# Triangular inverses of an RWKV-7 trunk layer: blocks of 16 joined to 32 by TensorE in place of blocks of 32 by substitution

## The chip, the cores and the metric

The kernel runs on one core of one Trainium2 chip. The metric is the device time of one execution in microseconds (us); the kernel before was run three times. Names of engines: TensorE (PE, with its weight loads as PEld), VectorE (DVE), ScalarE (ACT), GpSimd (POOL), SyncE (SP, which issues the DMAs).

## What is computed

One layer of a hybrid trunk on 128 context tokens and 512 latent tokens, width 1024: an input projection, a bidirectional RWKV-7 time mixing with 8 heads of 64 beside a grouped-query attention with 8 heads of 64, one output projection, and a gated feed-forward with a convolution of width 3. What this case is about is the time mixing:

```python
def wkv_scan(r, w, k, v, kk, a, s0, reverse):
    def step(s, inp):
        r_t, w_t, k_t, v_t, kk_t, a_t = inp
        sa = jnp.einsum('bhvk,bhk->bhv', s, -kk_t)
        s = (s * w_t[:, :, None, :]
             + sa[..., None] * (kk_t * a_t)[:, :, None, :]
             + v_t[..., None] * k_t[:, :, None, :])
        return s, jnp.einsum('bhvk,bhk->bhv', s, r_t)
```

It runs once forwards and once backwards over the tokens. The outputs are the two token streams, the new keys and values of the context and the final states.

## The kernel before

The scan is done in chunks of 64 tokens. Within a chunk the step's rank-one corrections form a strictly triangular 64 x 64 matrix L for each chunk, head and direction, and the chunk needs the inverse of (1 - L). The rest of a chunk is matmuls. There are three groups of such matrices: G0 and G1, each two pairs of heads over the 8 latent chunks, and CX, all four pairs over the 2 context chunks. A "unit" is one chunk and pair in one direction; a group has `nu` units per direction, 16 in G0 and G1 and 8 in CX. Two heads of a pair lie on partitions 0 to 63 and 64 to 127, so the tile `LT` of a group is 128 partitions x 32 units x 64.

`inverse` (L829) does a group in three stages:

- Blocks onto rows. Each 64 x 64 matrix has two diagonal blocks of 32. VectorE transposes in four instructions (L845), one per 32 partitions, so that each partition holds one unit's block of 32 x 32. L854 adds the block to its transpose, so that forward and backward units look alike.
- Substitution. L870 and L871 make the inverse of the 32 x 32 blocks, all 128 at once, column by column: 30 pairs of a product and a sum. They run on VectorE for G0 and CX and on POOL for G1 (`EN_INV`). Twelve small ScalarE copies (L858 to L864) set the start. Two VectorE transposes (L875, L877) bring the inverses back as `XT` and `XN`.
- Join to 64. TensorE makes W = L X and B = X W with matmuls of 32 x 32 x 32, each in its own quarter of rows (L897, L898, L909, L910), and copies put the blocks into `MT`.

The work around it: the front (`s_lora`, `s_kk`, `s_prep`, `s_bonus`) makes decays and keys beside the input projection (`s_gemm`, L502 and L521); `s_prep` ends with the matmuls `lt` (L819) and their masked copies into `LT` (L823). Then `s_gemm2` does the gate (L556) and the q projections (L570) while `s_gram`, `s_decay` and `s_chain` (L1042 to L1115) run the two scan directions; attention (`s_norm`, `s_scores`, `s_attn`) begins when the q projections and the inverse of G1 are through. The scans and the attention share TensorE; then come the output projection and the feed-forward.

What sets the order: every such function is a stream. `Flow` (L272) is a planner that takes, step by step, the stream that can start first by its estimated costs (`T` for TensorE, `V`, `A`, `G`) and priorities, with rings that count free PSUM banks; each `yield` names an engine and a cost. The order that comes out is fixed in the program, and each engine works through its own in order. PSUM rings used here: `mi` (2 banks; front, grams and decays, and the inverse of G0), `md` (1 bank), `tm` (3 banks; gate and q projections).

Of the kernel before, what the change touches and what calls it, by code (L numbers as in the profile page):

```python
# [9 lines left out]
F32 = mybir.dt.float32  # L10
# [3 lines left out]
ALU = mybir.AluOpType  # L14
# [5 lines left out]
P = 128  # L20
# [27 lines left out]
def trunk(ctx: ExitStack, tc: tile.TileContext, a, o, dbg=None):  # L48
# [8 lines left out]
    def nm(s):  # L57
        uid[0] += 1
        return f"{s}_{uid[0]}"
# [62 lines left out]
    qkn = rc.tile([P, 2, 64], F32, name="qkn")  # L122
    gnw = rc.tile([P, 4, 64], F32, name="gnw")
    bia = cst.tile([P, 4], F32, name="bia")
# [93 lines left out]
    sy.dma_start(qkn, a["qkn"].to_broadcast([P, 2, 64]))  # L218
    for h in range(2):
        sy.dma_start(gnw[64 * h:64 * h + 64], a["gnw"][h:h + 1].to_broadcast([64, 4, 64]))  # L220
    e2 = [psa.two("b2", "fm") for _ in range(2)]
# [50 lines left out]
    class Flow:  # L272
# [12 lines left out]
        def ring(f, name, n):  # L285
            f.rings[name] = [f.now] * n
# [95 lines left out]
    def ev_(*key):  # L382
        return ("ev", key)
# [444 lines left out]

    def inverse(g, en, pl, mp, sfx, rg, bank):  # L829
        eng = ve if en == "V" else ge  # L830

        def W(n, k=1):
            return V(n, k=k) if en == "V" else G(0.99 * (k * 0.1 + 2.2e-3 * n))
# [5 lines left out]
        yield ring("inv" + sfx)  # L839
        Lt = pl.tile([P, 1024], F32, name=nm("Lt"), tag="i0" + sfx)  # L840
        for qd in range(4):
            pr = slice(32 * qd, 32 * qd + 32)
            t0 = 32 * (qd % 2)
            yield V(1024)
            ve.transpose(Lt[pr].rearrange("p (t s) -> p t s", s=32), LT[pr, :, t0:t0 + 32].rearrange("p u t -> p t u"))  # L845
        Ls = pl.tile([P, 32, 32], F32, name=nm("Ls"), tag="i1" + sfx)
        X = pl.tile([P, 1024], F32, name=nm("X"), tag="i2" + sfx)
        X3 = X.rearrange("p (t s) -> p t s", s=32)
        Lt3 = Lt.rearrange("p (t s) -> p t s", s=32)
        yield G(1.0)  # L850
        ge.memset(X, 0.0)
        ge.memset(X[:, ::33], 1.0)
        yield W(1024)
        eng.tensor_tensor(Ls, Lt3, Lt3.rearrange("p t s -> p s t"), ALU.add)  # L854

        yield A(496, k=12)
        Lf = Ls.rearrange("p t s -> p (t s)")
        se.copy(X[:, 32::66], Lf[:, 32::66])  # L858
        for i in range(2):
            for j in range(2):  # L860
                se.copy(X[:, 64 + 32 * i + j::132], Lf[:, 64 + 32 * i + j::132])
        for b in (4, 8, 16):
            for q in range(0, 32, 2 * b):
                se.copy(X3[:, q + b:q + 2 * b, q:q + b], Ls[:, q + b:q + 2 * b, q:q + b])  # L864
        tmp = pl.tile([P, 256], F32, name=nm("tmp"), tag="i3" + sfx)
        for s in range(1, 31):
            n = 31 - s
            yield W(2 * n * s, k=2)
            t3 = tmp[:, :n * s].rearrange("p (t j) -> p t j", j=s)
            eng.tensor_tensor(t3, Ls[:, s + 1:32, s:s + 1].to_broadcast([P, n, s]), X3[:, s:s + 1, 0:s].to_broadcast([P, n, s]), ALU.mult)  # L870
            eng.tensor_tensor(X3[:, s + 1:32, 0:s], X3[:, s + 1:32, 0:s], t3, ALU.add)  # L871
        XT = pl.tile([P, 1024], F32, name=nm("XT"), tag="i0" + sfx)
        XN = pl.tile([P, 1024], F32, name=nm("XN"), tag="i1" + sfx)
        yield V(1024)
        ve.transpose(XT, X)  # L875
        yield V(1024)
        ve.transpose(XN.rearrange("p (j u) -> p j u", u=32), X3.rearrange("p i j -> p j i"))  # L877
        XT3 = XT.rearrange("p (i u) -> p u i", u=32)
        XN3 = XN.rearrange("p (j u) -> p u j", u=32)
        MT = mp[0].tile([P, 2 * nu, 64], F32, name=nm("MT"), tag=mp[1] or "MT" + g.nm)  # L880
        g.MT = MT
# [616 lines left out]
    weights = [flow.add(3, s_wload(1, jobs1 + jobs2, wpool, 2), 0), flow.add(3, s_wsplit(1, jobs1 + jobs2, wpool, 2), 0)]  # L1498
    flow.add(1.2, inverse(G0, "V", ri, (ri, None), "", "mi", mi), B_I0)
    flow.run([flow.add(2, s_gemm())])  # L1500
# [36 lines left out]
    for d in range(2):  # L1537
        rwkv += [flow.add(pri, st_(d), {s_chain: B_CH, s_load: 200, s_gram: 100, s_decay: 50}[st_]) for pri, st_ in ((0, s_chain), (0.1, s_load), (0.2, s_gram), (0.2, s_decay))]
    flow.add(PR_INV[0], inverse(CX, EN_INV[0], ri, (rp2, None), "", "md", md), B_INV)
    ipp = pool("ip", side="left")  # L1540
    inv1 = flow.add(PR_INV[1], inverse(G1, EN_INV[1], ipp.__enter__(), (ri, "LTg0"), "x", "md", md), B_INV)
    rwkv += [flow.add(0.5, s_setup(), 100), flow.add(0.75, s_final(), B_FIN)]
# [673 lines left out]
```

## Time and profile before

| | |
|---|---|
| runs | 1106.88, 1106.60, 1103.13 us; median 1106.6 |
| the profiled execution | 1104.36 us |
| its span, first to last instruction | 1102.6 us |
| TensorE busy | 1019.5 us (92%), mean granted clock 0.94 |
| VectorE busy | 790.7 us (72%) |
| ScalarE busy | 563.4 us (51%) |
| POOL busy | 507.4 us (46%) |

An engine's busy time is the union of its instructions; matmuls are pipelined and their ends are modelled, so a busy TensorE is not always one at its peak. The granted clock is TensorE's: 1.00 is 2.4 GHz, 0.50 is 1.2 GHz, and a mean between mixes the two. A matmul of f32 operands stands in the trace as two records. The columns of each view are named where it first appears.

### The profile page before, as it was taken

The numbers are of one execution on the slowest core, as the hardware profiler recorded it, in microseconds if no ns is written. First come the engines' busy times: TensorE is split into PE (matmuls) and PEld (weight loads), VectorE is DVE, ScalarE is ACT, GpSimd is POOL, SyncE is SP. The second block draws the span as 40 slices with busy tenths as digits, with TensorE's granted clock in tenths as the row PEclk, the third lists the DMA queues.
The fourth block names the chain that finished last, engine by engine and source line by source line (L and its number), as shares of the span: only waits on it lengthen the run. The fifth ranks groups of instructions, "written<-read, shape, count | busy, mean of one in ns | idle before, by whom it ended". The sixth has DMA issues, their size and how long they took to land. (4 is left out here: it accounts for less than half of the span.)

```text
span 1102.6 us, 20567 instructions
## 1 busy us (share of the span) xinstructions
PE 1019.5 (92%) x8034; PEld 853.6 (77%) x8034; DVE 790.7 (72%) x1367; ACT 563.4 (51%) x1261; POOL 507.4 (46%) x446
## 2 busy tenths in 40 slices
PE   6999998778779999999999988999999998899997
PEld 3788776677665556777777888999999997788885
DVE  3536689989729777465774789999999999643324
ACT  4275433254654767476654764555555556334431
POOL 1234423567415204210202058788888888642330
PEclk8899998889857899799999999999999999899999
DMA  9414534640245684211061421222222223531202
GB/s 364 185 67 116 152 103 133 184 126 21 97 150 194 212 267 136 68 59 61 9 229 74 153 90 44 88 89 94 77 77 78 78 99 112 193 113 58 95 1 96
DMA packets 70433, 127.84 MB, mean 116 GB/s; under 512 B 15664, under 2 KB 41776, under 8 KB 67264
## 3 DMA queue, kind: packets, MB, share of 16 engines
q1 hardware_dynamic: 70336, 126.53, 34.4%
q8 instruction: 63, 1.03, 0.4%
q14 instruction: 34, 0.28, 0.1%
HBM read 105.00 MB, written 21.51 MB: 115 GB/s over the span
## 5 line engine op out<-in xcount | busy, mean ns | idle before, releaser
L1807 POOL TENSOR_TENSOR w<-raw,w 128x512 fp32r<-128x512 f32 (+1 forms) x84 | 153.9, 1839 | 142.6 <-ACT w L1806 121.4
L2050 PE MATMUL dn<-w,ah 128*128 128x512 f32 x660 | 155.7, 398 | 7.9 <-DVE c L1850 7.9
L2050 PEld LDWEIGHTS dn<-w,ah 128*128 128x128 f32 x660 | 125.1, 190 | 38.3 <-issue 8.3
L1844 PE MATMUL up<-tq,w 128*128 128x324 f32 x960 | 150.2, 312 | 2.8 <-DVE x L1989 2.8
L1844 PEld LDWEIGHTS up<-tq,w 128*128 128x128 f32 x960 | 145.2, 190 | 3.1 <-DVE x L1989 3.1
L1844 PE MATMUL up<-hq,w 128*128 128x324 f32 x864 | 137.0, 313 | 4.8 <-ACT w L1806 2.3
L1844 PEld LDWEIGHTS up<-hq,w 128*128 128x128 f32 x864 | 129.6, 188 | 7.8 <-DVE up L1992 4.6
L1807 POOL TENSOR_TENSOR w<-sw,w 128x512 fp32r<-128x512 f32 x80 | 122.4, 1551 | 8.6 <-ACT w L1806 8.6
L1924 DVE TENSOR_TENSOR ah<-act,ah 128x644 fp32r<-128x644 f32 x42 | 58.7, 1415 | 75.8 <-ACT ah L1923 75.8
L1848 ACT ACTIVATE c<-up,pv 128x322 f32<-128x322 f32 x86 | 52.1, 620 | 97.3 <-DVE up L1992 55.6
L432 POOL TENSOR_TENSOR lo<-raw,hi 128x1024 fp32r<-128x1024 f32 x17 | 42.7, 2509 | 68.4 <-ACT hi L430 66.9
L1063 POOL TENSOR_TENSOR SP<-vse,pt 64x128 f32<-64x128 f32 x36 | 14.3, 398 | 128.4 <-DVE vse L1113 127.7
L1923 ACT CAST ah<-act 128x644 fp32r<-128x644 f32 x44 | 31.8, 732 | 76.4 <-PE dn L2050 76.3
L1806 ACT CAST w<-raw 128x512 fp32r<-128x512 f32 (+1 forms) x86 | 63.2, 748 | 5.0 <-PE dn L2050 2.8
L964 PE MATMUL gr<-AK 64*128 64x128 f32 x320 | 47.4, 329 | 11.8 <-ACT DT L377 4.5
L964 PEld LDWEIGHTS gr<-AK 64*128 64x128 f32 x320 | 38.8, 222 | 21.4 <-ACT DT L377 4.7
L1687 PE MATMUL op<-wo,m 128*128 128x512 f32 x192 | 48.3, 404 | 1.7 <-DVE m L1681 1.0
L1849 DVE SCALAR_TENSOR_TENSOR c<-up,pv,c 128x322 f32<-128x322 f32 x86 | 46.5, 543 | 3.8 <-ACT c L1848 3.8
L1806 ACT CAST w<-sw 128x512 fp32r<-128x512 f32 x80 | 47.5, 620 | 2.7 <-PE up L1844 2.7
L1850 DVE SCALAR_TENSOR_TENSOR c<-up,pv,c 128x322 f32<-128x322 f32 x86 | 46.6, 545 | 0.8
L1687 PEld LDWEIGHTS op<-wo,m 128*128 128x128 f32 x192 | 36.7, 194 | 10.5 <-DVE m L1681 1.4
L968 DVE TENSOR_TENSOR GM<-gr,cm 128x512 f32<-128x512 f32 x40 | 26.8, 684 | 21.7 <-PE gr L964 21.3
(335 smaller groups left out, 2485.1 us busy)
## 6 DMA issues: line engine op xcount, KB each, us to landing
wm<-in_wmod SPq DMA_DIRECT2D x24, 1024.0 KB, 6.6
raw<-in_up SPq DMA_DIRECT2D x44, 512.0 KB, 3.3
raw<-in_down SPq DMA_DIRECT2D x22, 512.0 KB, 3.3
AK<-arkd SPq DMA_DIRECT2D x40, 256.0 KB, 4.4
raw<-in_wfm SPq DMA_DIRECT2D x10, 512.0 KB, 5.9
arkd<-AR SPq DMA_DIRECT2D x8, 640.0 KB, 3.7
xT<-in_xT SPq DMA_DIRECT2D x8, 320.0 KB, 6.1
arkd<-BK SPq DMA_DIRECT2D x16, 160.0 KB, 3.5
```

What stands on the lines that cost most here:

```text
L432: ge.tensor_tensor(lo, raw, hi.bitcast(F32), ALU.subtract)
L964: te.matmul(ps[par][:, s, i], lhsT=ak[pr, i, 1], rhs=ak[pr, i, 0], start=True, stop=True)
L1687: te.matmul(acc[hf], lhsT=m2[xi][:, k - k0], rhs=wo[k // 2][wi][k % 2][:, 512 * hf:512 * hf + 512], start=(n_mm == 0 and pi == 0), stop=(n ...
L1806: se.copy(hi, raw)
L1807: eng.tensor_tensor(lo, raw, hi.bitcast(F32), ALU.subtract)
L1844: te.matmul(ps, lhsT=wq[wi][:, 128 * k:128 * k + 128], rhs=xq[xi][:, k], start=(first and k == 0 and pi == 0), stop=(last and k == 3 and p ...
L1848: se.activation(c, src[..., 1:H2N - 1], AF.Identity, scale=pv[:, col + 1:col + 2], bias=pv[:, col + 3:col + 4])
L1849: ve.scalar_tensor_tensor(c, src[..., 0:H2N - 2], pv[:, col:col + 1], c, ALU.mult, ALU.add)
L1850: ve.scalar_tensor_tensor(c, src[..., 2:H2N], pv[:, col + 2:col + 3], c, ALU.mult, ALU.add)
L1923: se.copy(t[:, 0, 1:645], act[:, k, 1:645])
L1924: eng.tensor_tensor(t[:, 1, 1:645], act[:, k, 1:645], t[:, 0, 1:645].bitcast(F32), ALU.subtract)
L2050: return [te.matmul(ps, lhsT=(ah, al)[xi][:, p0:p0 + 128], rhs=w2[wi][:, k % 2], start=(k == 0 and pi == 0), stop=(k == 21 and pi == 2)) f ...
```

## The change

The blocks that are inverted by substitution are now 16 x 16, two per old block of 32.

- Blocks onto rows: 128 matmuls per group (after.py L855) of 32 rows and 16 columns against a piece of the identity, in four quarters, into one PSUM bank `Lp`; ScalarE copies it (L863) and VectorE adds the transpose (L865), masks with a new constant `low` (L868) and sets the ones (L869).
- Substitution: 14 pairs (L875, L876), each on the two blocks of a partition at once.
- Join to 32: `T` (L895, L897), 4 matmuls per unit and direction; ScalarE copies `Ts` (L899); `D` (L911), 8 matmuls of 16 columns per unit and direction; VectorE adds them into `XN` and `XT` (L914, L915), the first through a row mask `m16`. The join to 64 stays.
- The second bank ring of an inverse is `mi` for G0 and `tm` for CX and G1.
- `low` lies where `gnw` lay; `gnw` is loaded in `s_final`, when `low` is free.

```diff
+    low = rc.tile([P, 4, 64], F32, name="low", tag="gnw").rearrange("p a (b s) -> p (a b) s", s=16)
+    ge.memset(low, 0.0)
+    for t in range(1, 16):
+        ge.memset(low[:, t, 0:t], 1.0)
+    m16 = rc.tile([P, 1], F32, name="m16")
+    ve.tensor_reduce(m16, ident.rearrange("p (q h x) -> p q h x", q=4, h=2)[:, :, 1], AX.XY, ALU.add)
...
-        for qd in range(4):
-            pr = slice(32 * qd, 32 * qd + 32)
-            t0 = 32 * (qd % 2)
-            yield V(1024)
-            ve.transpose(Lt[pr].rearrange("p (t s) -> p t s", s=32), LT[pr, :, t0:t0 + 32].rearrange("p u t -> p t u"))
...
+        quads = [(slice(32 * qd, 32 * qd + 32), slice(32 * qd, 32 * qd + 16), 32 * (qd % 2)) for qd in range(4)]
+        yield ring(rl)
+        Lp = lbank("Lt").rearrange("p (b t s) -> p b t s", b=2, s=16)
+        for t in range(32):
+            if t % 8 == 0:
+                yield T(0.6)
+            b = t // 16
+            for pr, _, t0 in quads:
+                c = pr.start + 16 * b
+                te.matmul(Lp[pr, b, t % 16], lhsT=LT[pr, :, t0 + t], rhs=ident[pr, c:c + 16], start=True, stop=True)
...
-        yield W(1024)
-        eng.tensor_tensor(Ls, Lt3, Lt3.rearrange("p t s -> p s t"), ALU.add)
-
-        yield A(496, k=12)
...
-        for s in range(1, 31):
-            n = 31 - s
-            yield W(2 * n * s, k=2)
...
+        yield A(512)
+        se.copy(Ls, Lp)
+        yield V(512)
+        ve.tensor_tensor(Ls, Ls, Lp.rearrange("p b t s -> p b s t"), ALU.add)
+        flow.give(rl)
+        yield V(544, k=2)
+        ve.tensor_tensor(Xb, Ls, low[:, None].to_broadcast([P, 2, 16, 16]), ALU.mult)
+        ve.memset(X[:, 0:1024:33], 1.0)
+        tmp = pl.tile([P, 112], F32, name=nm("tmp"), tag="i3" + sfx)
+        for s in range(1, 15):
+            n = 15 - s
+            yield W(4 * n * s, k=2)
...
+        Ts = pl.tile([P, 2 * nu, 32], F32, name=nm("Ts"), tag="i2" + sfx)
+        for h, rr, bb in ((0, rg, bank), (1, rl, lbank)):
+            yield ring(rr)
+            T3 = bb("T")[:, :32 * nu].rearrange("p (u j) -> p u j", j=32)
+            for u in range(h * nu, h * nu + nu):
+                if u % 8 == 0:
+                    yield T(0.5)
+                for pr, hr_, t0 in quads:
+                    if h:
+                        te.matmul(T3[pr, u - nu], lhsT=LT[pr, u, t0:t0 + 32], rhs=XT3[pr, u], start=True, stop=True)
+                    else:
+                        te.matmul(T3[pr, u], lhsT=LT[hr_, u, t0:t0 + 32], rhs=XN3[hr_, u], start=True, stop=True)
+            yield A(32 * nu)
+            se.copy(Ts[:, h * nu:h * nu + nu], T3)
+            flow.give(rr)
+        for h, rr, bb in ((0, rg, bank), (1, rl, lbank)):
+            yield ring(rr)
+            D3 = bb("D")[:, :32 * nu].rearrange("p (u w j) -> p u w j", w=2, j=16)
+            for u in range(h * nu, h * nu + nu):
+                if u % 8 == 0:
+                    yield T(1.0)
+                for pr, hr_, _ in quads:
+                    k = hr_ if h else pr
+                    ops = (((Ts[k, u], XN3[k, u, 0:16]), (XN3[k, u], Ts[k, u, 16:32])) if h else ((XT3[k, u], Ts[k, u, 0:16]), (Ts[k, u], XT3[k, u, 16:32])))
+                    for w, (l_, r_) in enumerate(ops):
+                        te.matmul(D3[pr, u - h * nu, w], lhsT=l_, rhs=r_, start=True, stop=True)
+            us = slice(h * nu, h * nu + nu)
+            yield V(32 * nu, k=2)
+            ve.scalar_tensor_tensor(XN3[:, us, 0:16], D3[:, :, 0], m16, XN3[:, us, 0:16], ALU.mult, ALU.add)
+            ve.tensor_tensor(XT3[:, us, 16:32], XT3[:, us, 16:32], D3[:, :, 1], ALU.add)
+            flow.give(rr)
...
+        gnw = rc.tile([P, 4, 64], F32, name="gnw", tag="gnw")
+        for h in range(2):
+            sy.dma_start(gnw[64 * h:64 * h + 64], a["gnw"][h:h + 1].to_broadcast([64, 4, 64]))
```

The order moves in three places that matter here. In these rows a name is that of a tile, "x16" counts equal instructions, and the shape at the end is that of the output.

TensorE at the end of the front, before: after the last piece of the k and v projection (`tm`) come the LT matmuls of the last head pair and then the gate (`fm`).

```order
L521 MATMUL tm_1814<-hi_1827,hhi 128x256
L521 MATMUL tm_1814<-hi_1827,hlo 128x256
L521 MATMUL tm_1814<-lo_1828,hhi 128x256
L819 MATMUL lt_1666<-AR_1606,BK_1607 64x64 x16
L819 MATMUL lt_1707<-AR_1606,BK_1607 64x64 x4
L819 MATMUL lt_1721<-AR_1661,BK_1662 64x64 x16
L819 MATMUL lt_1747<-AR_1661,BK_1662 64x64 x4
L556 MATMUL fm_2143<-hhi,hi_2025 128x320
```

The same place now (L518 is the projection, L816 `lt`, L734 the decays' matmul `lo`):

```order
L518 MATMUL tm_2445<-hi_2449,hlo 128x256
L518 MATMUL tm_2445<-lo_2450,hhi 128x256
L897 MATMUL T_1513<-XN_1456,LT_507 32x32 x64
L895 MATMUL T_1600<-XT_1455,LT_507 32x32 x64
L911 MATMUL D_1679<-Ts_1512,XT_1455 32x16
L911 MATMUL D_1679<-XT_1455,Ts_1512 32x16
```

Behind these two rows stand 126 more of D, then the LT matmuls of the third head pair, four of `lo` and the second 128 of D; only then the LT matmuls of the last pair. The join of G0 has moved ahead of the last two pairs' LT.

VectorE in the same stretch, now: the last pair of the substitution of G0, the two transposes, the join, and then the copies of the next LT matmuls (L820) and the products of the last pair (L792, L799).

```order
L876 TENSOR_TENSOR X_1331<-X_1331,tmp_1379 128x2x14
L880 STREAM_TRANSPOSE XT_1455<-X_1331 128x1024
L882 STREAM_TRANSPOSE XN_1456<-X_1331 128x1024
L914 SCALAR_TENSOR_TENSOR XN_1456<-D_1679,m_539,XN_1456 128x16x16
L915 TENSOR_TENSOR XT_1455<-XT_1455,D_1679 128x16x16
L820 SCALAR_TENSOR_TENSOR LT_508<-lt_1826,cm 128x8x64
L820 SCALAR_TENSOR_TENSOR LT_509<-lt_1862,cm 128x2x64
L792 TENSOR_TENSOR AR_1958<-E_1878,kk_1595 128x10x64
L799 TENSOR_TENSOR AR_1958<-E_1878,r_1500 128x10x64
```

Before, the copies and products stood between pairs of the substitution; now they stand behind instructions that wait for TensorE's D.

TensorE where the first scan step begins, before (`gr` a gram, `cp` the scan, `dt` a transpose, `tm` the q projections):

```order
L964 MATMUL gr_2152<-AK_2126 128x128 x4
L1067 MATMUL cp_2114<-vse_2134,GM_2150 64x64
L998 MATMUL dt_2369<-cm_76,BD_2153 128x128 x2
L570 MATMUL tm_3027<-lo_2383,hhi 128x256
L570 MATMUL tm_3027<-hi_2382,hhi 128x256
```

The same place now (L1104 is the scan's first matmul, L911 the join of CX):

```order
L911 MATMUL D_3106<-XT_2992,Ts_3002 32x16
L1104 MATMUL cp_2607<-vse_2627,GM_2643 64x64
L911 MATMUL D_3106<-Ts_3002,XT_2992 32x16
L1104 MATMUL cp_2607<-vso_2628,GM_2643 64x64
L911 MATMUL D_3106<-XT_2992,Ts_3002 32x16
L1104 MATMUL cp_2607<-vse_2627,GM_2643 64x64
L911 MATMUL D_3106<-Ts_3002,XT_2992 32x16
L1104 MATMUL cp_2607<-vso_2628,GM_2643 64x64
L911 MATMUL D_3106<-XT_2992,Ts_3002 32x16
```

Where the q projections stood, there are now joins, one matmul of the join between two of the scan. All 240 matmuls of the q projections come later: ahead of the first stand 8 of the scan's 160 first matmuls (L1067, now L1104), where none stood, and ahead of the last 60, where 20 stood.

## Rows read from the trace of the kernel before

**Rows 1.** The page's head and slices: 40 equal slices, busy share in tenths

```profile
span 1102.6 us, 20567 instructions
...
PE   6999998778779999999999988999999998899997
...
DVE  3536689989729777465774789999999999643324
...
POOL 1234423567415204210202058788888888642330
PEclk8899998889857899799999999999999999899999
```

**Rows 2.** Busy time by stage; columns as named in the first row

```profile
core 0: us, PE busy (x) PEld busy (x) DVE busy (x) ACT busy (x) POOL busy (x), PEclk, DMA share, GB/s
145.00:204.00 59.00, 54.86 (x436) 42.67 (x434) 55.51 (x82) 20.59 (x47) 19.77 (x11) 0.94 0.44 131
204.00:254.00 50.00, 36.72 (x555) 35.12 (x556) 45.67 (x50) 22.35 (x61) 35.20 (x44) 0.83 0.54 140
254.00:302.00 48.00, 38.56 (x457) 33.49 (x456) 41.55 (x73) 23.68 (x64) 26.90 (x46) 0.93 0.18 61
302.00:345.00 43.00, 37.13 (x520) 27.04 (x519) 20.81 (x42) 22.50 (x57) 9.16 (x16) 0.56 0.45 147
345.00:375.00 30.00, 26.63 (x285) 16.24 (x281) 24.09 (x70) 18.93 (x61) 15.94 (x30) 0.83 0.60 220
375.00:420.00 45.00, 42.99 (x433) 24.95 (x425) 34.68 (x88) 27.05 (x87) 5.25 (x11) 1.00 0.69 218
...
470.00:520.00 50.00, 49.00 (x596) 38.66 (x593) 31.98 (x80) 35.20 (x113) 6.37 (x16) 0.97 0.18 59
520.00:585.00 65.00, 63.29 (x622) 48.51 (x620) 44.15 (x126) 38.62 (x102) 10.72 (x24) 1.00 0.33 121
```

**Rows 3.** Waits of TensorE, 145 to 375 us: total us, times, longest us

```profile
PE lt L819 <- DVE LT L823: 6.7, 1, 6.7
PE gr L964 <- ACT DT L377: 4.5, 1, 4.5
PE dt L998 <- DVE GM L968: 4.2, 4, 1.7
PE gr L964 <- DVE GM L968: 3.5, 2, 3.3
PE cp L1089 <- ACT uvo L1080: 3.4, 1, 3.4
```

**Rows 4.** Groups of VectorE, 145 to 300 us: busy us, mean ns | idle before

```profile
L871 DVE TENSOR_TENSOR X<-X,tmp 128x30 f32<-128x30 f32 (+14 forms) x60 | 34.7, 578 | 2.4 <-ACT X L864 0.6
L870 DVE TENSOR_TENSOR tmp<-Ls,X 128x30 f32<-128x30 f32 (+14 forms) x60 | 28.1, 469 | 1.6
L845 DVE STREAM_TRANSPOSE Lt<-LT 32x1024 f32<-32x1024 f32 x12 | 23.8, 1982 | 0.2
...
L854 DVE TENSOR_TENSOR Ls<-Lt 128x1024 f32<-128x1024 f32 x2 | 4.3, 2160 | 0.0
```

**Rows 5.** Timeline of TensorE (start, us, line): W's first and last record; clock windows

```profile
222.50 0.22 PE L897 MATMUL W<-XN,LT 32*32 32x32 f32 x1
...
224.27 0.23 PE L898 MATMUL W<-XT,LT 32*32 32x32 f32 x1
...
315.21 0.26 PE L897 MATMUL W<-XN,LT 32*32 32x32 f32 x1
...
317.01 0.24 PE L898 MATMUL W<-XT,LT 32*32 32x32 f32 x2
...
222.40:224.40 2.00, 2.00 (x134) 1.92 (x132) 1.99 (x2) 1.98 (x3) 0.00 (x0) 1.00 1.04 394
...
315.20:317.20 2.00, 2.00 (x132) 1.92 (x130) 0.00 (x0) 0.27 (x1) 0.00 (x0) 0.50 0.94 347
```

**Rows 6.** Timeline of TensorE: 20 matmuls of one column

```profile
197.04 1.33 PE L718 MATMUL bo<-pv,kd 64*64 64x1 f32 x40
```

**Rows 7.** Timeline of TensorE: four scan matmuls alone, and one B between two

```profile
310.28 0.69 PE L1075 MATMUL cp<-Rt,MT 64*64 64x64 f32 x8
...
322.34 0.47 PE L1075 MATMUL cp<-Rt,MT 64*64 64x64 f32 x2
322.74 0.31 PE L909 MATMUL B<-XT,Ws 32*32 32x32 f32 x2
322.98 0.47 PE L1075 MATMUL cp<-Rt,MT 64*64 64x64 f32 x2
```

More of the change, by code (lines that the diff above doesn't have):

```diff
@@ L122, in trunk @@
     qkn = rc.tile([P, 2, 64], F32, name="qkn")
-    gnw = rc.tile([P, 4, 64], F32, name="gnw")
     bia = cst.tile([P, 4], F32, name="bia")
@@ L218, in trunk @@
     sy.dma_start(qkn, a["qkn"].to_broadcast([P, 2, 64]))
-    for h in range(2):
-        sy.dma_start(gnw[64 * h:64 * h + 64], a["gnw"][h:h + 1].to_broadcast([64, 4, 64]))
     e2 = [psa.two("b2", "fm") for _ in range(2)]
@@ L827, in s_prep, with inverse @@
             flow.done("ab", p, d)
-    def inverse(g, en, pl, mp, sfx, rg, bank):
+    low = rc.tile([P, 4, 64], F32, name="low", tag="gnw").rearrange("p a (b s) -> p (a b) s", s=16)
[4 more added lines that the diff above has]
+    ve.tensor_reduce(m16, ident.rearrange("p (q h x) -> p q h x", q=4, h=2)[:, :, 1], AX.XY, ALU.add)
+    def inverse(g, en, pl, mp, sfx, rg, bank, rl, lbank):
         eng = ve if en == "V" else ge
@@ L839, in inverse @@
         yield ring("inv" + sfx)
-        Lt = pl.tile([P, 1024], F32, name=nm("Lt"), tag="i0" + sfx)
-        for qd in range(4):
-            pr = slice(32 * qd, 32 * qd + 32)
-            t0 = 32 * (qd % 2)
-            yield V(1024)
-            ve.transpose(Lt[pr].rearrange("p (t s) -> p t s", s=32), LT[pr, :, t0:t0 + 32].rearrange("p u t -> p t u"))
-        Ls = pl.tile([P, 32, 32], F32, name=nm("Ls"), tag="i1" + sfx)
-        X = pl.tile([P, 1024], F32, name=nm("X"), tag="i2" + sfx)
-        X3 = X.rearrange("p (t s) -> p t s", s=32)
@@ L849, in inverse @@
-        Lt3 = Lt.rearrange("p (t s) -> p t s", s=32)
+        quads = [(slice(32 * qd, 32 * qd + 32), slice(32 * qd, 32 * qd + 16), 32 * (qd % 2)) for qd in range(4)]
[8 more added lines that the diff above has]
+                te.matmul(Lp[pr, b, t % 16], lhsT=LT[pr, :, t0 + t], rhs=ident[pr, c:c + 16], start=True, stop=True)
@@ L850, in inverse @@
+        Ls = pl.tile([P, 2, 16, 16], F32, name=nm("Ls"), tag="i1" + sfx)
+        X = pl.tile([P, 1056], F32, name=nm("X"), tag="i2" + sfx)
+        Xb = X.rearrange("p (b r) -> p b r", b=2)[:, :, :512].rearrange("p b (t s) -> p b t s", s=32)[:, :, :, 0:16]
+        X3 = X[:, :1024].rearrange("p (t s) -> p t s", s=32)
         yield G(1.0)
         ge.memset(X, 0.0)
-        ge.memset(X[:, ::33], 1.0)
-        yield W(1024)
-        eng.tensor_tensor(Ls, Lt3, Lt3.rearrange("p t s -> p s t"), ALU.add)
@@ L856, in inverse @@
-        yield A(496, k=12)
[L857 to L865, printed above, removed]
-        for s in range(1, 31):
-            n = 31 - s
-            yield W(2 * n * s, k=2)
-            t3 = tmp[:, :n * s].rearrange("p (t j) -> p t j", j=s)
-            eng.tensor_tensor(t3, Ls[:, s + 1:32, s:s + 1].to_broadcast([P, n, s]), X3[:, s:s + 1, 0:s].to_broadcast([P, n, s]), ALU.mult)
-            eng.tensor_tensor(X3[:, s + 1:32, 0:s], X3[:, s + 1:32, 0:s], t3, ALU.add)
+        yield A(512)
@@ new lines, in inverse @@
+        se.copy(Ls, Lp)
[9 more added lines that the diff above has]
+            yield W(4 * n * s, k=2)
+            t3 = tmp[:, :2 * n * s].rearrange("p (b t j) -> p b t j", b=2, j=s)
+            eng.tensor_tensor(t3, Ls[:, :, s + 1:16, s:s + 1].to_broadcast([P, 2, n, s]), Xb[:, :, s:s + 1, 0:s].to_broadcast([P, 2, n, s]), ALU.mult)
+            eng.tensor_tensor(Xb[:, :, s + 1:16, 0:s], Xb[:, :, s + 1:16, 0:s], t3, ALU.add)
@@ L874, in inverse @@
         yield V(1024)
-        ve.transpose(XT, X)
+        ve.transpose(XT, X[:, :1024])
         yield V(1024)
@@ L1498, in trunk @@
     weights = [flow.add(3, s_wload(1, jobs1 + jobs2, wpool, 2), 0), flow.add(3, s_wsplit(1, jobs1 + jobs2, wpool, 2), 0)]
-    flow.add(1.2, inverse(G0, "V", ri, (ri, None), "", "mi", mi), B_I0)
+    flow.add(1.2, inverse(G0, "V", ri, (ri, None), "", "mi", mi, "mi", mi), B_I0)
     flow.run([flow.add(2, s_gemm())])
@@ L1516, in trunk @@
     psq = Banks("psq", tm=3)
+    tm = lambda s: psq.one("tm", s)
     flow.ring("tm", 3)
@@ L1538, in trunk @@
         rwkv += [flow.add(pri, st_(d), {s_chain: B_CH, s_load: 200, s_gram: 100, s_decay: 50}[st_]) for pri, st_ in ((0, s_chain), (0.1, s_load), (0.2, s_gram), (0.2, s_decay))]
-    flow.add(PR_INV[0], inverse(CX, EN_INV[0], ri, (rp2, None), "", "md", md), B_INV)
+    flow.add(PR_INV[0], inverse(CX, EN_INV[0], ri, (rp2, None), "", "md", md, "tm", tm), B_INV)
     ipp = pool("ip", side="left")
-    inv1 = flow.add(PR_INV[1], inverse(G1, EN_INV[1], ipp.__enter__(), (ri, "LTg0"), "x", "md", md), B_INV)
+    inv1 = flow.add(PR_INV[1], inverse(G1, EN_INV[1], ipp.__enter__(), (ri, "LTg0"), "x", "md", md, "tm", tm), B_INV)
     rwkv += [flow.add(0.5, s_setup(), 100), flow.add(0.75, s_final(), B_FIN)]
```

## The prediction

> **What bounds the kernel now.** I read four views in this order: the slices of the page, a table of busy time by stage, what TensorE waited for, and the order of TensorE's instructions where the inverses stand. The slices [rows 1] show that no one engine bounds the whole program: VectorE is at 8 and 9 tenths in slices 6 to 10, about 138 to 276 us, which is where the three inverses run, and TensorE dips to 7 and 8 in slices 7 to 12, where from slice 13 on it is at 9. The stage table [rows 2] says the same in numbers. Between 145 and 302 us VectorE is busy for 142.7 of 157 us and TensorE for 130.1, at a mean clock of 0.94, 0.83 and 0.93. From 302 to 375 us VectorE is free, but TensorE has a stretch at 0.56 of its clock, which is almost all the lower of its two levels, 1.2 GHz. From 375 us on (scans and attention together) TensorE is busy 42.99 of 45, 49.00 of 50 and 63.29 of 65 us at full or nearly full clock. So behind 375 us there is little left to fill, and the scans and the attention go as fast as TensorE's queue lets them. What happens before is different: the idle times of the first five rows add up to 4.1 + 13.3 + 9.4 + 5.9 + 3.4 = 36 us, and the missing clock, (1 - clock) times busy, to 3.3 + 6.2 + 2.7 + 16.3 + 4.5 = 33 us. These 69 us are all that a better filled TensorE could get back.
>
> The waits [rows 3] say who holds TensorE there: VectorE, late with masks and copies, for 6.7 + 4.2 + 3.5 us and a few smaller ones, 17 us in all; ScalarE for another 17 us (4.5 and 3.4 are the longest), some of it waiting for VectorE itself.
>
> **What the change takes away.** On VectorE it removes 12 transposes of L845 (23.8 us) and the two sums of L854 (4.3 us), and 64 of the 120 instructions of L870 and L871, which took 62.8 us [rows 4]; the 56 left are the short ones, so at most 28/60 of the time stays, 29 us. That is at least 62 us. It adds per inverse four operations of 256 to 544 elements and the four joins, some 3 us, 10 us in all. On POOL the second half of the group G1 shrinks in the same way. So VectorE loses some 50 of the 143 us that filled it. Twelve short ScalarE copies per inverse give way to three longer ones, which I count as even. The 16 memsets of the mask and the one reduction come once, at the program's start, where POOL is at 1 tenth [rows 1]: nothing, and if that cover were gone a few us. The load of gnw moves to the final part; in SP's queue it now waits until the last inverse has read the mask, with a weight load and later AK loads behind it. The weights behind it are wanted only once the inverses of TensorE's queue are through, so I cost it at nothing; if not, the q projections are late.
>
> **What it adds on TensorE.** First, matmuls of 32 rows: per full group 128 for the blocks onto rows, 128 for T and 256 for D, for the context group 128 + 64 + 128. That is 512 + 512 + 320 = 1344, where there were 320. None of 16 columns is in the trace. The nearest rows are W, 32 by 32 by 32 [rows 5]: 64 of them, 128 records, start within 1.77 us, 29 ns each, at clock 1.00, and within 1.80 us at clock 0.50. A price that the clock doesn't touch is not one of streamed columns, and even with one column a matmul (L718, 20 of them in 1.33 us, [rows 6]) costs 66 ns. So I take 29 ns for all: 1344 x 29 ns = 39 us. The bound below is half for the 1024 of 16 columns, 9 + 15 = 24 us.
>
> On this the Trainium skill, "TensorEngine Tiling (Array Packing)", section Instruction Overhead, says that a matmul with one moving column has the latency of one with 60. By it 16 columns are no cheaper than 32 and the term stays at 39 us; without it the sum would be 15 us lower. No row here shows 16 columns.
>
> Second, changes between 32-row matmuls and others. The planner interleaves the streams, and in the order there are 74 runs of 32-row matmuls where there were 16, 42 of them a single matmul between two of the scan. That is 148 changes instead of 32. The one place where the trace shows such a mix is B with the scan [rows 7]: from one scan matmul to the next with one B matmul between, 0.64 us. Four scan matmuls alone take 0.69 us at the same clock, so 0.17 each; less 0.03 for the B, 0.44 us is left for two changes, 0.22 us each at half clock. At full clock no row shows it; half of that, 0.11 us, is the bound. 116 more changes cost 13 to 26 us; I take 0.17, since the clock in this stretch lies between, 20 us.
>
> Together 59 us of TensorE time, all in front of the stage that is full.
>
> **What it gives back.** The 17 us for which VectorE held TensorE go, and half of the 17 that ScalarE did, 8 us. What is late next is the joins: TensorE works in order, D stands behind T and waits for ScalarE's copies, VectorE's joins wait for D, and behind them on VectorE stand the copies of LT and the products of the last head pair, so the last LT matmuls and with them the end of the front come no sooner, although the substitution itself is done early. The other half of ScalarE's waits (copies into MT, which stay) therefore stays. Of the 33 us of missing clock I take half, 15: the gaps that made the clock fall get shorter, but the new matmuls and the changes are the very kind of work during which it was low [rows 5, 7]. Given back: 17 + 8 + 15 = 40 us.
>
> **The sum.** The profiled execution took 1104.4 us, its span 1102.6. 1104.4 + 39 + 20 - 40 = 1123 us. The median of the runs, 1106.6, lies 2 us above that execution, which I leave in the noise but round up for: **1124 us**.
>
> **The rivals.**
> - *VectorE was the bound and the rest follows (faster).* For it: VectorE busy for 91% of 157 us [rows 2], and the first row of the waits. Against it: TensorE was itself busy for 83% of that time. It wins if the 16-column matmuls cost half and TensorE gets back three quarters of its 69 us: 24 + 13 - 52 = -15, **1089 us**. The point from which it decides: what TensorE gets back must pass what is added, 37 to 65 us.
> - *No change.* Added and given back meet, for instance 39 + 13 - 52. **1104 us**, within 5 us.
> - *The clock stays low (slower still).* Small matmuls between waits in order, a change at each, and the q projections scattered among them: only 20 us come back, 39 + 26 - 20 = +45, **1149 us**. For it: the stretch at 0.56 is just where W, B and the scans were mixed. Against it: in 254 to 302 us the same kinds of work ran at 0.93.
> - That the substitution isn't shortened can be left aside: the order has 28 instructions in the place of 60.
>
> **How the numbers follow.** The forecast (added work, over half of the slack back, 1110 to 1140 us) has 0.45, the low clock 0.15, no change 0.15, faster 0.25. I put weight on faster because the prices for 16 columns and for a change at full clock are both taken from far rows and both err to the dear side if they err. The range goes from 1089 to 1149 us: it leaves out about half of each outer case, 2 in 10. A measurement of this kernel can tell about 0.5%, 5.5 us, from no change. Slower by more: 0.45 + 0.15 = 0.60; within: 0.15; faster: 0.25. The forecast case alone has 1110 to 1140 us.
>
> **What would show it.** Right: 32-row matmuls at about 29 ns from start to start, at either clock; changes of 0.1 to 0.2 us; VectorE at 6 tenths or less between 145 and 300 us; the q projections (L570) ending some 50 us or more later than before, with more scan steps done by then; TensorE's busy time up by some 40 us, and the stage from scans to attention ending about 20 us later. Wrong: TensorE's queue idle for less than 15 us between 145 us and the end of the q projections, at full clock, or a join that costs under 10 us per group; then it comes out faster. It is wrong the other way if the mean clock stays under 0.8 up to that point.

## The result and the profile after

| | before | changed |
|---|---|---|
| median of the runs | 1106.4 us (4 runs, 1103.1 to 1106.9) | 1199.6 us (4 runs, 1198.3 to 1204.2) |
| span of the profiled execution | 1102.6 us | 1197.7 us |
| ratio, 95% interval | | 1.086 (1.082 to 1.089) |

The change makes the kernel slower by 93 us. The direction was forecast, the size was not: 1124 us was predicted, and the time lies 50 us above the range.

The slices of the changed kernel answer to [rows 1]. VectorE (DVE) is no longer full in slices 6 to 10, and TensorE (PE) is not fuller for it: its clock is at 5 to 6 tenths in slices 7 to 12.

```profile
span 1197.7 us, 25887 instructions
...
PE   6999997769999998789977899999999999799997
...
DVE  4545755442112247976854457999999999663423
...
POOL 2143542223002114631100202988888888573330
PEclk8899997656669989768999999999999999899999
```

The stages, to be read beside [rows 2]:

```profile
core 0: us, PE busy (x) PEld busy (x) DVE busy (x) ACT busy (x) POOL busy (x), PEclk, DMA share, GB/s
145.00:204.00 59.00, 55.18 (x899) 45.63 (x897) 32.91 (x49) 21.58 (x38) 21.77 (x11) 0.90 0.43 124
204.00:254.00 50.00, 30.57 (x1157) 26.75 (x1151) 15.97 (x24) 15.88 (x23) 13.14 (x12) 0.57 0.51 133
254.00:302.00 48.00, 43.30 (x936) 36.66 (x937) 21.04 (x51) 17.82 (x47) 13.55 (x33) 0.61 0.13 43
302.00:345.00 43.00, 43.00 (x984) 35.29 (x981) 5.89 (x13) 12.17 (x32) 2.39 (x6) 0.58 0.10 34
345.00:375.00 30.00, 28.84 (x488) 25.68 (x487) 8.46 (x15) 15.78 (x41) 0.80 (x2) 0.92 0.15 51
...
470.00:520.00 50.00, 38.76 (x369) 28.25 (x369) 44.00 (x96) 27.31 (x89) 33.22 (x43) 0.70 0.31 94
520.00:585.00 65.00, 62.38 (x686) 49.05 (x682) 41.09 (x105) 42.93 (x133) 10.63 (x23) 0.84 0.09 32
585.00:620.00 35.00, 28.77 (x220) 20.45 (x216) 26.18 (x67) 18.88 (x47) 1.17 (x8) 0.95 0.26 87
620.00:666.00 46.00, 34.24 (x258) 23.16 (x258) 20.03 (x39) 21.01 (x49) 0.00 (x0) 1.00 0.05 16
```

VectorE has 33 instead of 56 us in the first row and 6 instead of 21 in the fourth. TensorE's idle time from 145 to 375 us falls from 36 to 29 us only, and its missing clock, (1 - clock) times busy, rises from 33 to 56 us: from 204 to 345 us it stays near 0.5 and 0.6, mostly on the lower level of 1.2 GHz. Behind 375 us, where it was full before, it now has room: 470 to 520 us and 585 to 666 us (in the last two rows it was busy for 33.3 of 35 and 42.9 of 46 us before).

What TensorE waited for between 145 and 375 us is another list than [rows 3]. The waits for VectorE and ScalarE are all but gone. At the top stands "issue", time in which it waited for nothing that the profile shows:

```profile
PE D L911 <- issue: 8.3, 5, 3.7
PE Lt L855 <- issue: 7.9, 5, 2.0
PE B L946 <- issue: 5.0, 1, 5.0
PE W L934 <- issue: 2.4, 1, 2.4
PE T L895 <- issue: 1.3, 1, 1.3
PE T L897 <- DVE XN L882: 1.0, 1, 1.0
```

These 25 us of stops all lie in runs of 32-row matmuls; the kernel before has no such row for TensorE there. The timeline shows their rhythm where the blocks of CX come onto rows (start, us, line, records, idle before). Each stretch of 128 records, 64 matmuls, takes 2.01 us, and then TensorE stops for 1.4 to 2 us:

```profile
250.31 2.01 PE L855 MATMUL Lt<-cm,LT 32*32 32x16 f32 x128 [1.55 <-issue]
254.31 2.02 PE L855 MATMUL Lt<-cm,LT 32*32 32x16 f32 x128 [1.99 <-issue]
258.04 2.02 PE L855 MATMUL Lt<-cm,LT 32*32 32x16 f32 x128 [1.71 <-issue]
261.49 0.86 PE L855 MATMUL Lt<-cm,LT 32*32 32x16 f32 x44 [1.43 <-issue]
```

The view of the DMAs from 249 to 263 us, in 40 slices of 0.35 us, shows the same rhythm with nothing else on the queues:

```profile
GB/s 0 0 0 0 0 0 47 0 0 0 0 0 0 0 0 0 0 0 0 47 0 0 0 0 0 0 0 0 0 47 0 0 0 0 0 0 0 0 0 47
...
q8 instruction: 4, 0.07, 1.9%
```

Four packets of instructions, 16 KB each (47 GB/s for 0.35 us), 3.5 to 4.5 us apart. On the page this queue has 84 packets and 1.38 MB, where the kernel before has 63 and 1.03. The 21 more for 1344 matmuls are 64 matmuls a packet: with two passes, each a weight load and a matmul, 4 instructions per matmul and 256 per packet. So a long run of small matmuls waits for its own instructions. The rest of the trace bears this out: the twelve longest stops, 24 of the 25 us, each end 1.3 to 1.6 us after one of these packets has landed. The Trainium skill, "Runtime: NRT & Kernel Launch", section Instruction fetch mechanics, has blocks of 16 KiB with 256 instructions, which agrees with these numbers; it also calls their cost mostly hidden, and here it is not: 3.7 us pass per packet, of which 2.0 are work.

The second thing that stands out is attention. Its first scores and the last of the q projections before, and then in the changed kernel (line, form, count, ns, first and last start):

```profile
L1408 PE MATMUL s<-K,qs x16: 272/275/327, 383.9 to 494.4; 128*128 128x128 f32 x16
L570 PE MATMUL tm<-lo,hhi x80: 274/283/562, 226.4 to 302.1; 128*128 128x256 f32 x80
```

```profile
L1448 PE MATMUL s<-K,qs x16: 272/371/454, 537.5 to 607.1; 128*128 128x128 f32 x16
L567 PE MATMUL tm<-lo,hhi x80: 278/283/415, 298.0 to 427.3; 128*128 128x256 f32 x80
```

The projections end 125 us later and attention begins 154 us later, while the scan (its last first-matmul at 583.0, before 547.4) ends 36 us later. From 585 us on attention runs alone.

Third, the inverses themselves. G0's substitution is through earlier, as its last transpose shows, before and after:

```profile
219.54 2.04 DVE L877 STREAM_TRANSPOSE XN<-X 128x1024 f32<-128x1024 f32 x1
```

```profile
195.54 1.97 DVE L882 STREAM_TRANSPOSE XN<-X 128x1024 f32<-128x1024 f32 x1
```

That is 24 us won. But the last B matmul of G0 ends at 248.4 us, before at 232.4, and that of G1 at 367.4, before at 330.5.

### The profile page after: what moved, and what is told of

Read it like the earlier page. It is cut to its first block, busy times and chain, and to the rows that moved or that the text cites. A ratio compares the mean times of both kernels' runs of the same rounds, so it can differ in the third digit from the quotient of the medians.

```text
span 1197.7 us, 25887 instructions
## 1 busy us (share of the span) xinstructions
PE 1092.6 (91%) x10722; PEld 913.7 (76%) x10722; DVE 725.7 (61%) x1302; ACT 571.7 (48%) x1243; POOL 486.7 (41%) x426
## 3 DMA queue, kind: packets, MB, share of 16 engines
q8 instruction: 84, 1.38, 0.5%
## 5 line engine op out<-in xcount | busy, mean ns | idle before, releaser
L1964 ACT CAST ah<-act 128x644 fp32r<-128x644 f32 x44 | 31.8, 731 | 76.6 <-PE dn L2091 76.5
L374 ACT COPY PT<-pt 128x512 f32<-128x512 f32 (+1 forms) x50 | 25.9, 518 | 40.3 <-PE pt L1479 40.2
```

Of the source, the lines that this page charges most:

```text
L1964: se.copy(t[:, 0, 1:645], act[:, k, 1:645])
```

## The experiments

Each time is the median of its runs, beside runs of the kernel before on the same chip (1103 to 1106 us). Where an expectation names "stops", the rows "issue" are meant. "Steps" counts the scan's 80 first steps that stand ahead of the last q projection in TensorE's order: 10 before, 30 in the change. Run 3 is read by its trace; its one execution took 1221.1 us.

| run | ratio, 95% interval | us | added matmuls | runs of small matmuls | steps |
|---|---|---|---|---|---|
| the change | 1.086 (1.082 to 1.089) | 1199.6 | 1344 | 74 | 30 |
| 1 q first | 1.054 (1.051 to 1.057) | 1164.8 | 1344 | 83 | 4 |
| 2 blocks by VectorE | 1.090 (1.086 to 1.094) | 1204.5 | 960 | 55 | 32 |
| 4 G1 as before | 1.086 (1.081 to 1.091) | 1199.3 | 832 | 33 | 32 |
| 5 q first, joins whole | 1.046 (1.040 to 1.052) | 1155.5 | 1344 | 16 | 4 |
| 6 before, q first | 1.034 (1.028 to 1.040) | 1141.4 | 0 | 46 | 0 |
| 7 as 5, blocks by VectorE | 1.039 (1.032 to 1.046) | 1148.3 | 960 | 16 | 4 |
| 8 joins whole | 1.071 (1.065 to 1.077) | 1182.1 | 1344 | 13 | 24 |
| 9 order like before | 1.055 (1.050 to 1.059) | 1165.5 | 1344 | 13 | 12 |
| 10 as 9, blocks by VectorE | 1.044 (1.038 to 1.050) | 1153.8 | 960 | 12 | 12 |
| 11 as 9, D twice | 1.100 (1.095 to 1.105) | 1214.9 | 1984 | 25 | 12 |
| 12 G1 alone | 1.029 (1.024 to 1.035) | 1137.8 | 512 | 9 | 12 |
| 13 before + idle matmuls | 1.046 (1.041 to 1.050) | 1151.7 | 1344 | 17 | 8 |
| 14 before, joins whole | 0.993 (0.990 to 0.996) | 1094.1 | 0 | 6 | 10 |

(The blocks by matmuls are 384, 128 for each group; the 320 in the expectations is a miscount.)

**1. The q projections first.**

```diff
-    gemm2 = flow.add(2, s_gemm2(), 100)
+    gemm2 = flow.add(0.05, s_gemm2(), 1000)
```

> The changed kernel with one number altered, so that the gate and the q projections stand ahead of the scan in TensorE's order (4 of the scan's 80 first steps before the last q projection, where the change has 30 and the kernel before 10). All 1344 added matmuls stay. Order theory: the loss of 93 us is there because attention waits for the q projections (first score at 537 us, was 384), so that it runs on alone after the scan; with the projections in front the first score comes before 430 us and the time falls to 1110 to 1140 us. Rival, work theory: TensorE's added work, its stops without anything waited for (25 us) and the low clock are the loss, and the order only decides who pays: 1175 to 1200 us.

1164.8 us: 35 us come back, and 60 stay. The first score is at 420.8 us. Neither theory alone holds.

**2. The blocks onto rows by VectorE.**

```diff
-                te.matmul(Lp[pr, b, t % 16], lhsT=LT[pr, :, t0 + t], rhs=ident[pr, c:c + 16], start=True, stop=True)
...
+            ve.transpose(Lt[pr].rearrange("p (t s) -> p t s", s=32), LT[pr, :, t0:t0 + 32].rearrange("p u t -> p t u"))
```

> The changed kernel with the blocks brought onto rows by VectorE's four transposes per group again, as before; the substitution of blocks of 16 and the joins T and D stay. 320 small matmuls less, and VectorE has 24 us more. In the order the q projections still stand behind 32 of the scan's 80 first steps. Order theory: attention is still late, 1185 to 1200 us. Work theory: 320 matmuls at 29 ns are 9 us, at 57 ns (with the stops) 18 us, so 1180 to 1190 us, and less if the clock comes back.

1204.5 us, and the first score stays at 533 us. As long as attention starts so late, 384 matmuls less buy nothing.

**3. The prices by themselves.** Useless matmuls are appended to the kernel before; `dn` is their output and x1t, the last result, their input.

```diff
+            for q in range(4):
+                pr = slice(32 * q, 32 * q + 32)
+                te.matmul(m3[pr, u % (512 // cols)], lhsT=xs[pr, 32 * (u % 8):32 * (u % 8) + 32], rhs=xs[pr, 256 + cols * (u % 8):256 + cols * (u % 8) + cols], start=True, stop=True)
```

> The kernel before with matmuls put behind its last one, whose results nobody uses: 384 of 32x32 with 32 columns, 384 with 16 columns, 384 of 64x64 with 64 columns, then 64 pairs of two 64-row matmuls and 64 pairs of a 64-row and a 32-row one in turn. As predicted before: 29 ns each for the first two blocks (11 us each) at any clock and 0.1 to 0.2 us for a change. Supply theory: after each 64 matmuls (256 instructions of TensorE, and the page shows 21 more instruction packets of 16 KB for 1344 more matmuls, which is 64 per packet) TensorE stops for 1.4 to 2 us with nothing waited for, 57 ns each, 22 us a block, for 16 columns as for 32; at 64 rows and columns too, if they are issued as fast. If the price is one of columns, the second block takes half of the first.

The 384 of 32 columns run from 1103.66 to 1124.8 us, 55 ns each, and the 384 of 16 columns from there to 1147.4, 59 ns each, at 128 records and a stop in turn:

```profile
1128.00 1.90 PE L2088 MATMUL dn<-x1t 32*32 32x16 f32 x128 [2.12 <-issue]
1131.47 1.90 PE L2088 MATMUL dn<-x1t 32*32 32x16 f32 x128 [1.57 <-issue]
1134.94 1.90 PE L2088 MATMUL dn<-x1t 32*32 32x16 f32 x128 [1.57 <-issue]
1138.69 1.90 PE L2088 MATMUL dn<-x1t 32*32 32x16 f32 x128 [1.85 <-issue]
1142.43 1.90 PE L2088 MATMUL dn<-x1t 32*32 32x16 f32 x128 [1.84 <-issue]
```

Behind the first stop one packet happened to run at the full clock and the next at half of it (the clock is the third number from the end):

```profile
1108.70:1110.10 1.40, 1.27 (x128) 1.16 (x128) 0.00 (x0) 0.00 (x0) 0.00 (x0) 1.00 0.05 12
1112.40:1114.40 2.00, 1.93 (x128) 1.79 (x128) 0.00 (x0) 0.00 (x0) 0.00 (x0) 0.50 0.03 8
```

So the 64 matmuls themselves are faster at the full clock, 1.27 us against 1.93. But each of these two packets starts 3.7 us ahead of the next, so the faster one only has the longer stop.

The page has 85 instruction packets, 22 more than before, and 1408 matmuls were added: again 64 a packet. The 384 of 64 rows take 24.3 us, 63 ns each, with no stop. The clock of the three stretches (16 columns; 64 rows; a 64-row and a 32-row matmul in turn):

```profile
1130.00:1145.00 15.00, 7.60 (x512) 7.17 (x512) 0.00 (x0) 0.00 (x0) 0.00 (x0) 0.50 0.02 4
1150.00:1170.00 20.00, 20.00 (x675) 20.00 (x672) 0.00 (x0) 0.00 (x0) 0.00 (x0) 0.97 0.02 4
1190.00:1205.00 15.00, 15.00 (x96) 10.75 (x96) 0.00 (x0) 0.00 (x0) 0.00 (x0) 0.50 0.00 0
```

While small matmuls run and stop, the clock is on its lower level, 1.2 GHz; in the even block of 64 rows it is back at 2.4. The block of small and other matmuls in turn began at 1.00 and ran at 0.50 from 1182 us on, with TensorE busy all the time:

```profile
1199.82 0.47 PE L2102 MATMUL dn<-x1t 64*64 64x64 f32 x2
1200.22 0.31 PE L2103 MATMUL dn<-x1t 32*32 32x32 f32 x2
1200.46 0.47 PE L2102 MATMUL dn<-x1t 64*64 64x64 f32 x2
```

From one pair to the next are 0.64 us, what [rows 7] showed with B and the scan. Less 0.11 us for the 64-row matmul, its price at 0.50 in the block before (from start to start), and 0.03 for the small one, a change costs 0.25 us at 1.2 GHz, a little more than the 0.22 forecast. The first pairs of the block stood at the full clock, for which the prediction had no row:

```profile
1179.10:1181.70 2.60, 2.60 (x27) 1.92 (x25) 0.00 (x0) 0.00 (x0) 0.00 (x0) 1.00 0.00 0
1179.13 0.24 PE L2103 MATMUL dn<-x1t 32*32 32x32 f32 x2
1179.30 0.33 PE L2102 MATMUL dn<-x1t 64*64 64x64 f32 x2
1179.56 0.24 PE L2103 MATMUL dn<-x1t 32*32 32x32 f32 x2
```

From pair to pair are 0.43 us. A 64-row matmul among others like it takes 0.06 us at this clock; less that and 0.02 to 0.03 us for the small one, a change costs 0.17 us, not half of 0.22. Supply theory holds for 32 and for 16 columns, and a price by columns is out.

**4. G1 as before.**

```diff
-    inv1 = flow.add(PR_INV[1], inverse(G1, EN_INV[1], ipp.__enter__(), (ri, "LTg0"), "x", "md", md, "tm", tm), B_INV)
+    inv1 = flow.add(PR_INV[1], inverse_old(G1, EN_INV[1], ipp.__enter__(), (ri, "LTg0"), "x", "md", md), B_INV)
```

> The changed kernel with the last group, G1, inverted as before (substitution of blocks of 32 on POOL); G0 and the context group stay changed. 512 small matmuls less, 33 runs of small matmuls instead of 74, and hardly any single ones between matmuls of the scan. In the order the q projections still stand behind 32 of the scan's 80 first steps. Order theory: attention is still late, 1180 to 1200 us. Work theory: 512 x 57 ns = 29 us and some 80 changes at 0.2 us = 16 us come back: 1150 to 1160 us.

1199.3 us with 512 matmuls and 82 changes less, first score at 531 us: the order theory's figure, like run 2.

**5 to 8. Order, changes, control.** Run 5 has the edit of run 1 and this one, run 7 those of 1 and 2 and this one, run 8 this one alone; run 6 is the edit of run 1 in the kernel before.

```diff
-    B_CH, B_FIN, B_INV = 200, 0, 100
+    B_CH, B_FIN, B_INV = 200, 0, 1000
```

> The q projections first, and the inverses of CX and G1 with so high a priority that their matmuls stand in one piece each: 16 runs of small matmuls, none of a single matmul, where the run with the q projections first had 83, 48 of them single. The work is the same. Changes theory: 134 fewer changes at 0.17 us are 23 us, and the clock no longer falls between them: 1120 to 1145 us. Supply theory: in one piece the small matmuls outrun the fetch of their instructions, 57 instead of 29 ns each, so what the changes give back is lost in stops: 1155 to 1170 us, with 15 us or more of stops without anything waited for.

1155.5 us, 9 less than run 1, and 24 us of stops at lines of the blocks and joins, where run 1 has 16. Once joins are in one piece they outrun their instructions, as supply theory had it.

> Control: the kernel before, with the gate and the q projections first in the same way. If the order of the q projections matters only where the change upset it, the time stays at 1104 us within 6 us; if the placing was simply not the best one, it falls below 1098 us, and the gain of 35 us seen in the changed kernel says less of the change.

1141.4 us, 36 us slower, which neither case allowed for. The trace shows where it comes from: the q projections now stand ahead of G0's joins in TensorE's order. The last B of G0 ends at 282.7 us (before 232.4), VectorE stands idle for 41.6 us until then, and the scan's first step comes at 295 to 298 us (before 247 to 252). From 302 to 345 us TensorE is busy for 31.8 of 43 us at a clock of 0.52: the q projections, spent too early, are missing there. So "first" is not the undoing of "late", and run 1 may understate what lateness costs.

> The q projections first, the joins in one piece, and the blocks onto rows by VectorE's transposes: of the change remain the short substitution and the joins T and D, 1024 small matmuls more than before. Against the run with the q projections first and whole joins 320 small matmuls less. Supply theory: 320 x 57 ns = 18 us less than that run. If VectorE holds the inverses up again (24 us of transposes), the two are equal within 6 us. By neither theory is it faster than 1104 us: 1024 x 57 ns = 58 us of TensorE, less the 36 us of idle time of before: 1115 to 1145 us.

1148.3 us, 7 less than run 5: neither the 18 of supply theory nor equal within 6. It is a little above the range given, and slower than before, as expected.

> The changed kernel with the inverses of CX and G1 in one piece and the q projections left late (24 of the scan's 80 first steps before the last; the change has 30): 13 runs of small matmuls where the change has 74. Changes theory: 120 fewer changes at 0.17 us, 20 us: about 1180 us. Order theory: attention still starts at about 530 us and the time stays at 1190 to 1205 us.

1182.1 us, 17 less than the change, the figure of the changes theory. But the first score is at 500 us and not at 530, so this run does not separate the changes from the place of the q projections.

**9 to 12. An order like before.** Run 9 has the edit of run 8 and a middle value for the q projections; 10 adds the edit of run 2, 11 issues every D twice, 12 uses the new inverse for G1 alone.

```diff
-    gemm2 = flow.add(2, s_gemm2(), 100)
+    gemm2 = flow.add(2, s_gemm2(), 1000)
```

> All of the change, with the small matmuls of CX and G1 in one piece each (13 runs, none single) and the q projections about where they stood before: 12 of the scan's 80 first steps before the last one, where the kernel before has 10. What is left against 1105 us is then the price of 1344 matmuls in place of VectorE's work. At 29 ns each and all of it on the path: 39 us, 1144 us. At 57 ns (with the stops for instructions): 77 us, less what VectorE gives back: 1150 to 1170 us. If order is all, 1105 to 1120 us.

1165.5 us, within the range for 57 ns: 60 us remain when the changes are gone and the steps are like before. Attention is still later than before, with its first score at 464 us (before 384). Against run 8 (24 steps), 17 us are the later q projections.

> The same with the blocks onto rows by VectorE's transposes: 320 small matmuls less, VectorE 24 us more; again 12 of 80 scan steps before the last q projection. Supply theory: 18 us less than with the matmuls (9 us at 29 ns). If VectorE is what holds the front up, 10 to 20 us more instead.

12 us less. For the 384 matmuls that it really saves the two prices are 22 and 11 us, so the lower one is met, VectorE's 24 us included; VectorE with 24 us more does not hold the front up.

> The run with the order like before, with each matmul of the join D issued twice: 640 small matmuls more, whose result is the same. At 29 ns each: 19 us more. At 57 ns: 36 us more, with some 10 more stops of 1.4 to 2 us at lines of the join. If the joins were hidden beside other work: nothing.

49 us more, 77 ns for each added matmul, more than either price, with few stops: 4 us at D, where run 9 has 14. In D two matmuls in a row go to the same quarter of rows; doubled, it is four in a row, and each output is written twice. The second half of G0's D takes 234.5 to 251.1 us where run 9 has 223.2 to 228.4 us, so 11.4 us more for 128 matmuls, 89 ns each. The joins are not hidden, which was the question; as a price per matmul the run says little, since a doubled matmul isn't one more of the same kind and there are 24 more changes.

> Only the last group, G1, is inverted in the new way (its substitution on POOL); G0 and CX as in the kernel before; the q projections with 12 of 80 scan steps before the last, 9 runs of small matmuls. 512 small matmuls more than before. At 57 ns on the path: 29 us, 1134 us; at 29 ns 15 us, 1120 us. If only the joins ahead of the scan's first step cost, G0's and CX's, the time is 1105 us within 8 us.

33 us more than before for 512 matmuls, 64 ns each. So G1's joins are not hidden, though the scan's first step doesn't wait for them. The 64 ns are not their price alone: attention's first score comes at 443.9 us, 60 later than before.

**13 and 14. The other side of the sum.** Run 13 adds useless matmuls to the kernel before, run 14 is the edit of run 8 in it.

```diff
+        D3 = bank("D").rearrange("p (u j) -> p u j", j=32)
+        for z in range(128 if nu == 16 else 80):
...
+                te.matmul(D3[pr, z % 16], lhsT=LT[pr, z % (2 * nu), 0:32], rhs=XT3[pr, z % (2 * nu)], start=True, stop=True)
```

> The kernel before with 1344 small matmuls put in one piece per group between the substitution and W (512, 320 and 512), whose results nobody uses; VectorE and POOL keep all of their work, and the order is otherwise that of before (8 of the scan's 80 first steps before the last q projection, before 10; 17 runs of small matmuls, before 16). It is the added work without what it buys. The run with the whole change in an order like before took 60 us more than before. If VectorE's 50 us less were worth the 40 us that were forecast, this run takes 40 us more than that one: 1195 to 1215 us. If they were worth nothing: 1155 to 1175 us. At 57 ns each the matmuls alone are 77 us: 1182 us, a relief of 17 us.

1151.7 us, 14 us less than run 9. The same number of matmuls costs less with VectorE's work left in than with it taken out. The two runs differ in more than that: here the results are waited for by nothing but one copy, and the q projections end at 316.4 us, in run 9 at 380.8. The first row of TensorE's waits in this run, 145 to 385 us:

```profile
PE D L898 <- issue: 33.7, 17, 4.8
```

The 17 stops add up to 34 us; the run is 49 us slower than before. Each of them ends 1.2 to 1.5 us after an instruction packet has landed.

> The kernel before with the matmuls of CX's and G1's joins in one piece each: 6 runs of small matmuls where there are 16, 20 changes fewer, the order else the same. Changes theory: 20 x 0.14 to 0.17 us are 3 us less, 1101 to 1103 us, the only version of the study that would be no slower than before. If a change costs only where the clock is low, nothing.

1094.1 us, 0.7% faster than before: the one version here that beats both, and by more than the 3 us expected. The 8 us would be 0.4 us for each of the 20 changes, more than run 3 shows, but they are not shown to be the changes'. In the two profiles some of the gain lies where no small matmul runs: from 420 to 470 us the clock is at 0.93 with TensorE busy for 48.3 us, before at 0.82 and 46.8.

## Why the prediction was wrong

**The bound** was read rightly as far as the runs go: none shows VectorE's load to set the time. Run 10 gives VectorE 24 us more to do than run 9, with 384 matmuls less, and is 12 us faster. Of VectorE's relief nothing is left to see: the added matmuls cost 49 us with VectorE's work left in (run 13) and 60 with it taken out (run 9). No run has the relief by itself.

**What the change takes away** was right, and even too careful: L875 and L876 now take 11.0 + 7.0 us (145 to 300 us) against 29 forecast. The DMA of gnw held nothing up, as said: it was issued at 265.0 us after a wait of 18.9, and the next weight load, at 279.2, had its own wait of 13.0 us for POOL.

**29 ns per small matmul: the first step that failed.** That 16 columns are no cheaper than 32 was right. That the clock plays no part was true of the row it came from [rows 5] but not of run 3, where 64 matmuls take 1.27 us at the full clock and 1.93 at half. The larger fault is that this row is a run of 64, just one packet of instructions. Longer runs go at 55 to 59 ns (run 3), so 1344 would be some 77 us of TensorE's time and not 39, an estimate. The order showed the new runs to be longer; the price was taken from a run too short to show the supply run dry. In run 13 the program pays 49 us for them, so part of that time replaces time that was lost before.

**The changes**, 20 us forecast for 116 of them at 0.17, were priced well as instructions: run 3 shows 0.17 us at the full clock and 0.25 at half. (The four scan matmuls of [rows 7] start 0.11 us apart; their 0.17 each contained the length of the last one, so 0.22 was too low.) What they cost the program is not separated. Run 8 has 122 fewer than the change and is 17 us faster, but its q projections also come sooner. From run 1 to run 5, 134 fewer give 9 us, with 8 us more of stops. Run 4 has 82 fewer, and 512 matmuls less, and gains nothing while attention is late.

**The 40 us given back: the step that failed worst.** The waits for VectorE and ScalarE did go. Stops took their place, so TensorE's idle time to 375 us fell by 7 us in place of 25, and the clock, from which 15 us were to come back, took 23 more. The text named what is late next, the joins, and then still booked the relief in full. The inverses show it: substitution 24 us earlier, inverse of G0 16 us later. Run 13 against run 9 leaves nothing of the 40: run 9 should be the faster by that much and is 14 us slower, of which the 4 steps between them may be some 6 (17 us for 12 steps, an estimate).

**The q projections' lateness** was forecast as a sign (50 us; it was 125) and entered in the sum at nothing. That sentence had its condition, "if not, the q projections are late", but the cause was the order and not the weights' queue, and no price was put on attention starting late. It is 17 us from 12 to 24 steps, with the joins whole (runs 9 and 8).

So, as differences between runs, the 93 us are: 60 that stay in run 9, 17 more from there to run 8 by late q projections, and 17 from run 8 to the change, by changes and 6 steps of lateness together. The 60 are not the matmuls' price alone, as attention is late in run 9 too. Still open: how they split between stops, issue, the clock that falls with them and attention's start.

**The rival "the clock stays low"** came nearest. It had the mechanism (0.57 to 0.61 from 204 to 345 us, and 0.76 on the mean from 145 us to the end of the q projections, below the mark of 0.8), with its price too small by half, since it too left out the stops and attention. Its chance of 0.15 rested on a misreading: that "the same kinds of work" ran at 0.93 from 254 to 302 us. That stretch holds 1.1 us of W, no B and 20.7 us of q projections; the stretches with B ran at 0.83 and 0.56. The stage that was called full leaves out a row as well: from 420 to 470 us the clock was at 0.82 before.

## What to carry to other kernels

Price a small instruction from a run as long as the new one will be: here 64 matmuls of f32 are one packet of instructions, the next 64 wait for another, and 29 ns become 55 to 59. Work that is moved from a full engine to one that bounds the program pays only if the chain behind it gets shorter; follow it to its last consumer, not to the step that was made faster. And where a planner sets the order, look at what the change pushes back: the same matmuls cost 60 or 93 us by the place of others.

## What the runs showed of the hardware

- TensorE's instructions come in packets of 16 KB, 64 small f32 matmuls each. A run of 32-row f32 matmuls uses one up in 1.9 to 2.0 us at 1.2 GHz (1.27 us at 2.4 GHz, run 3) and has the next 3.5 to 4.0 us after it began on the one before, with the DMA queues otherwise empty (the change, 249 to 263 us; run 3). At 63 ns per matmul of 64 rows there are no stops (run 3).
- Two matmuls in a row on each quarter of rows: 128 records in 1.80 us, 14 ns apart (D in run 9). Four in a row, each output written twice: 449 in 14 us, 31 ns apart (D in run 11). Both at 1.2 GHz.
- Runs with stops lie at the lower clock, 1.2 GHz (0.50 in run 3), and so do, after a beginning at 1.00, small matmuls in turn with others; an even block of 64-row matmuls right behind the stops is at 2.4 GHz (0.97).
- A change between a 64-row and a 32-row matmul costs some 0.25 us at 1.2 GHz and 0.17 us at 2.4 GHz, worked out from pairs 0.64 and 0.43 us apart (run 3).
